# Decoder trunk: one 512-column pass of each weight tile's high part over both activation parts

## Chip, core and metric

The kernel runs on one core of a Trainium2 chip. Its engines are TensorE (PE, with weight loads shown apart as PEld), VectorE (DVE), ScalarE (ACT), GpSimd (POOL) and SyncE (SP, which only issues DMAs here). Each takes its instructions in the order in which they stand on it; semaphores tie them together. The metric is the device time of one execution in microseconds, the median of several runs.

## What is computed

Two layers of a hybrid decoder block over 256 tokens of 1024 features, float32 in and out:

```python
def reference(x, mem, positions, ...):          # x (1, 256, 1024), mem (1, 256, 1024)
    for l in range(2):
        h = rmsnorm(x, norm_mix[l])
        x = x + mixer_block(h, ...)             # below
        x = x + cross_attention(rmsnorm(x, ...), rmsnorm(mem, ...), wq, wk, wv, wo)   # 4 heads
        x = x + squared_relu_mlp(rmsnorm(x, ...), w_up, w_down)                       # 4096 hidden
    return rmsnorm(x, norm_final)

def mixer_block(h, ...):
    zin = h @ w_in                              # 6840 columns: operands of four mixers, and gates
    o_a = mla_branch(...)                       # latent attention, causal
    o_b = spatial_gating_branch(...)            # gMLP
    o_c = gla_branch(...)                       # gated linear attention
    o_d = deltanet_branch(...)                  # short convolution, triangular solve
    proj = einsum('bsnw,nwd->bsnd', branches, w_branch)
    gate = sigmoid(gates).reshape(b, s, 4, 1024)
    return sum(gate * proj, axis=2) @ w_out
```

## The kernel before

**Products.** Activations lie feature-major: 128 features on the partitions, 256 tokens along the free axis, so that a weight tile of 128 x 128 is loaded into TensorE and 256 columns of activations pass over it. Every float32 operand is split into a high part that float32r holds exactly and a low part, the rest. `mm3` (L176 to L179) makes one product of three matmuls: high weights with high activations (L177), high weights with low activations (L178), low weights with high activations (L179). The low x low product is left out.

**Weights.** `half` (L156) hands out the weight stream: 1 MB loads by SyncE into three raw buffers, each of two halves; a half is eight tiles of 128 x 128. ScalarE rounds a half to `wh` (L172), VectorE subtracts to get `wl` (L173); four buffers of each.

**Loops.** `gemm` (L181) runs over pairs of blocks of 128 output features, and in a block over the k-tiles of 128 input features (8, or 32 in the MLP's down product). A pair shares one PSUM bank of three (`pg`, tiles named g). With `lead` the first pair, with `tail` the last pair goes into banks of their own. A function `evac` takes the result away: for the gates one ScalarE tanh over 512 elements (L1043), for the MLP's up product a VectorE maximum, a ScalarE square and a split (L1164 to L1174), for products that go back into `x` a VectorE add (L335), and for keys, queries and others a ScalarE copy and a VectorE subtraction (`split_ps`). `gemm_tok` makes token-major products with 512 columns per matmul.

**Memory.** Working tiles come from a pool of 44 pieces of 2080 bytes per partition. `new` takes the piece that has been free longest (`free.pop(0)`), `rel` puts it at the end of the list. This happens in the program's order; a tile's first write then waits for the last use of what was in its piece. The gates of the first four output blocks (`gates(0)` to `gates(3)`) have tiles of their own (`gate_tile`), those of the last four take pieces.

**Order.** The program is written layer by layer: input projection, then `soft_gates`, `conv`, the rest of the projection, then two chains that take turns (DeltaNet: `dn_system`, `dn_solve`, `dn_out`; and gMLP, MLA, GLA one after the other), then eight `gates(m)`, the operands of `mem`, the keys of the cross-attention (tiles kx), eight `merge(m)`, the output product, cross-attention and MLP. A list scheduler then sets the order of instructions on each engine: whatever is ready goes first, so matmuls of the gates, which need nothing from the mixers, are placed between the steps of the mixers' chains. `urgent` and the priorities `HP` and `WP` move some instructions ahead. That order is fixed when the program is built.

Names in the chains: `head_out` (L715) norms and gates a branch's output (`sq`, `rb`, small tiles dn..), `out_branch` (L409) splits it (`brh`, `brl`, L411 and L412). In GLA, `cum` holds cumulated decays, `dd` their differences (GpSimd L788, ScalarE L789), `kt` and `qt` the scaled keys and queries of seven levels, L827 the score products, L837 to L841 the masked copies into `sc`. In DeltaNet L622 to L648 is the solve, L658 to L691 the outputs.

Of the kernel before, what the change touches and what calls it, by code (L numbers as in the profile page):

```python
# [24 lines left out]
# columns of the combined input projection  # L25
# [15 lines left out]
# pieces of on-chip memory (2080 bytes per partition each)  # L41
N_PIECE = 44
# [3 lines left out]
# constants  # L46
# [7 lines left out]
def decoder(ctx: ExitStack, tc: tile.TileContext, ws, xt_d, mem_d, pos_d, nrm_d, par_d, cst_d, msk_d, out_d):  # L54
# [26 lines left out]
    free = list(range(N_PIECE))  # L81
    owner = {}

    def new(dt=F32, shape=(P, 2, T), name="a"):
        assert free, "no piece left: " + str(sorted(n for _, _, n in owner.values()))
        i = free.pop(0)
        t = ap.tile(list(shape), dt, tag=f"pc{i}", name=nm(name))
        owner[id(t)] = (i, t, name)
# [23 lines left out]
    hh = [cp.tile([P, 2, T], F32R, name=f"hh{j}") for j in range(4)]  # L112
    hl = [cp.tile([P, 2, T], F32R, name=f"hl{j}") for j in range(4)]
# [4 lines left out]
    # first loads: x between the parts of the first weights  # L118
# [62 lines left out]
    def gemm(xh, xl, nk, npair, evac, lead=False, tail=False):  # L181
        """feature-major product, two blocks of 128 output features at a time; evac gets (blocks, psum) parts.
        lead: the first two blocks go side by side, for operands that are still being made.
        tail: the last two blocks in banks of their own, to be taken one by one."""
        for p in range(npair):
            apart = (lead and p == 0) or (tail and p == npair - 1)
            if apart:
                bk = [pg.tile([P, 2, T], F32, tag="g", name=nm("g")) for _ in range(2)]
                parts = [(slice(m, m + 1), bk[m][:, 0:1]) for m in range(2)]
                out = [bk[m][:, 0] for m in range(2)]  # L190
            else:
                ps = pg.tile([P, 2, T], F32, tag="g", name=nm("g"))
                parts = [(slice(0, 2), ps)]
# [7 lines left out]
            for m, k in order:  # L201
# [3 lines left out]
                mm3(out[m], w[m][0][:, c], w[m][1][:, c], xh(k), xl(k), k == 0, k == nk - 1)  # L205
            evac(p, parts)

    def ch(tiles):
        return lambda k: tiles[k // 2][:, k % 2, :]

    def gemm_tok(xh, xl, evac):
        """token-major product with 512 columns: out[t] = x[t]^T w"""
        ps = [pg.tile([P, 512], F32, tag="g", name=nm("g")) for _ in range(2)]
        for f in range(4):
            wh, wl = half()
            for kk in range(2):
                k = 2 * f + kk
                c = slice(512 * kk, 512 * kk + 512)
                for t in range(2):
                    s = slice(128 * t, 128 * t + 128)  # L220
                    mm3(ps[t], xh(k)[:, s], xl(k)[:, s], wh[:, c], wl[:, c], k == 0, k == 7)
# [18 lines left out]
    def rsqrt2(src, scale, eps, name):  # L240
        """the same for two columns, as two chains that take turns"""
# [15 lines left out]
    def row_of(cols, out=None, name="row"):  # L257
        """columns [128, 2] (token-major) -> [128, 256], the same row on every partition"""
# [54 lines left out]
    def gate_tile(i, dt=F32, name="gt"):  # L313
        return ap.tile([P, 2, T], dt, tag=f"gt{i}", name=nm(name))

    def operands(j, g, mix=False, parts=(slice(0, 2),)):
        if mix and parts[0].start == 0:
            if j == 0:
                Norm.h, Norm.l = [], []
            Norm.h.append(gate_tile(2 * j, F32R, "xh")), Norm.l.append(gate_tile(2 * j + 1, F32R, "xl"))  # L320
        if g is not None:
            dh, dl = (Norm.h[j], Norm.l[j]) if mix else (hh[j], hl[j])
# [3 lines left out]
    def residual(g, mix=False, row=None):  # L326
        @urgent
        def evac(p, parts):
            for c, ps in parts:
                if row is not None:  # L330
                    t = new(name="rt")
                    V.tensor_tensor(t[:, c], ps, bc2(row, c.stop - c.start), op=ALU.mult)
                    ps = t[:, c]
                    rel(t)
                V.tensor_tensor(xs[p][:, c], ps, xs[p][:, c], op=ALU.add)  # L335
                operands(p, g, mix, (c,))
            sumsq(p, xs[p], [c for c, _ in parts], g is None)
            if g is None:
                Norm.xg = [new(name="xg")] if p == 0 else Norm.xg + [new(name="xg")]
                for c, _ in parts:  # L340
# [56 lines left out]
    def layer(l):  # L397
# [5 lines left out]
        # values that pass between the parts of a layer  # L403
# [3 lines left out]
        brh, brl = [None] * 4, [None] * 4  # L407

        def out_branch(n, src):  # L409
            brh[n], brl[n] = new(F32R, name="brh"), new(F32R, name="brl")  # L410
            S.copy(brh[n], src)  # L411
            V.tensor_tensor(brl[n], src, brh[n].bitcast(F32), op=ALU.subtract)  # L412

        H, L = ch(hh), ch(hl)
# [953 lines left out]
```

## Time and profile before

| | before |
|---|---|
| median of 3 runs | 1117.18 us (1116.73 to 1117.33) |
| span of the profiled execution, its first to its last instruction | 1114.9 us |
| mean granted TensorE clock | 0.996 |
| ScalarE busy | 588.4 us |
| GpSimd busy | 185.7 us |
| DMA | 184.68 MB, mean 166 GB/s |

The profiled execution has no time of its own beside its span; the median of the runs is 2.3 us longer than that span. L12 stands for line 12 of the kernel; a line can be that of a helper, so all feature-major products have the lines 177 to 179. `x105` counts instructions. A matmul's duration overlaps that of the next one, since matmuls are pipelined; float32 matmuls outside the products appear twice in the trace for one in the program.

### The profile page before, as it was taken

What the parts mean: (1) busy time and instruction counts of PE and PEld (TensorE: products, weight loads), DVE (VectorE), ACT (ScalarE), POOL (GpSimd) and SP (SyncE); (2) the same over time, 40 slices, a digit from 0 to 9 for tenths busy, and PEclk for the clock granted to TensorE, in tenths of its full rate; (3) what the DMA queues carried; (4) which work ended last, traced back from release to release, by engine and by line L of the source; (5) the groups of instructions that cost most, each with busy time, mean ns of one, the idle gap of its engine ahead of it and who ended that gap; (6) DMA issues with size and microseconds to landing.
All of it is one profiled execution on the core that took longest, in us unless ns stands there. A gap on an engine that the chain in (4) does not pass through costs nothing.

```text
span 1114.9 us, 21506 instructions
## 1 busy us (share of the span) xinstructions
PE 1095.4 (98%) x8894; PEld 1070.2 (96%) x8894; DVE 811.1 (73%) x1415; ACT 588.4 (53%) x883; POOL 185.7 (17%) x173
## 2 busy tenths in 40 slices
PE   7999999999999999999999999999999999999996
PEld 7999999999999999999999999999999899999996
DVE  6999858868875866655689996686796777665543
ACT  6575555644654655544455646545454555554441
POOL 2233014108200200000102320410450010000010
PEclk9999999999999999999999999999999999999998
DMA  8454424454543555555545343344555344555541
GB/s 318 176 190 149 152 77 142 162 171 170 190 151 114 192 187 189 188 180 183 180 176 200 136 162 140 107 150 160 178 180 178 147 145 165 184 187 189 190 152 38
DMA packets 28035, 184.68 MB, mean 166 GB/s; under 512 B 3488, under 2 KB 3744, under 8 KB 6560
## 3 DMA queue, kind: packets, MB, share of 16 engines
q1 hardware_dynamic: 26784, 181.19, 45.6%
q10 hardware_dynamic: 1152, 2.10, 0.7%
q8 instruction: 70, 1.15, 0.4%
q14 instruction: 29, 0.24, 0.1%
HBM read 182.23 MB, written 1.05 MB: 164 GB/s over the span
## 4 chain that ended last, share of the span: by engine, by line
PE 93%; DVE 4%; ACT 1%; issue 1%; DMA 0%; POOL 0%; SPq 0%; DVEq 0%
PE g L177 27%; PE g L178 27%; PE g L179 27%; PE ps L827 1%; DVE wl L173 1%; PE ps L177 1%; PE ps L178 1%; PE ps L179 1%; PE ps L622 1%; PE ps L626 1%; DMA x<-xt 0%; ACT wh L172 0%; PE ps L933 0%; DVE hn L449 0%; PE ps L742 0%
## 5 line engine op out<-in xcount | busy, mean ns | idle before, releaser
L173 DVE TENSOR_TENSOR wl<-wr,wh 128x1024 fp32r<-128x1024 f32 (+1 forms) x338 | 414.0, 1227 | 188.5 <-ACT wh L172 184.3
L172 ACT ACTIVATE wh<-wr 128x1024 fp32r<-128x1024 f32 (+1 forms) x338 | 355.0, 1053 | 363.8 <-PE g L178 314.1
L179 PE MATMUL g<-hh,wl 128*128 128x256 f32 x1280 | 363.8, 285 | 1.4 <-DVE wl L173 1.4
L177 PE MATMUL g<-hh,wh 128*128 128x256 f32 x1280 | 363.4, 285 | 0.0
L178 PE MATMUL g<-hl,wh 128*128 128x256 f32 x1280 | 362.9, 284 | 0.0
L179 PEld LDWEIGHTS g<-hh,wl 128*128 128x128 f32 x1280 | 245.0, 192 | 2.5 <-DVE wl L173 1.8
L178 PEld LDWEIGHTS g<-hl,wh 128*128 128x128 f32 x1280 | 245.3, 192 | 0.7 <-issue 0.5
L177 PEld LDWEIGHTS g<-hh,wh 128*128 128x128 f32 x1280 | 245.0, 192 | 0.6 <-issue 0.2
L178 PE MATMUL g<-al,wh 128*128 128x256 f32 x512 | 144.1, 281 | 0.0
L177 PE MATMUL g<-ah,wh 128*128 128x256 f32 x512 | 144.0, 281 | 0.0
L179 PE MATMUL g<-ah,wl 128*128 128x256 f32 x512 | 144.0, 281 | 0.0
L179 PEld LDWEIGHTS g<-ah,wl 128*128 128x128 f32 x512 | 96.5, 188 | 0.0
L177 PEld LDWEIGHTS g<-ah,wh 128*128 128x128 f32 x512 | 96.4, 188 | 0.0
L178 PEld LDWEIGHTS g<-al,wh 128*128 128x128 f32 x512 | 96.4, 188 | 0.0
L291 POOL TENSOR_TENSOR sq<-sq,sq 128x512 f32<-128x512 f32 x16 | 23.6, 1474 | 408.6 <-ACT sq L285 408.5
L177 PE MATMUL g<-xh,wh 128*128 128x256 f32 x160 | 46.2, 293 | 6.9 <-ACT wh L172 6.9
L1059 POOL TENSOR_TENSOR gt<-gt,gt 128x512 f32<-128x512 f32 x16 | 35.7, 2228 | 99.3 <-DVE gt L1058 98.4
L178 PE MATMUL g<-xl,wh 128*128 128x256 f32 x160 | 46.2, 291 | 0.7 <-DVE xl L271 0.7
L179 PE MATMUL g<-xh,wl 128*128 128x256 f32 x160 | 46.1, 290 | 0.0
L177 PEld LDWEIGHTS g<-xh,wh 128*128 128x128 f32 x160 | 31.5, 199 | 7.0 <-ACT wh L172 6.9
L1167 DVE TENSOR_SCALAR up<-g 128x512 f32<-128x512 f32 (+1 forms) x34 | 22.5, 660 | 20.8 <-PE g L179 20.6
L177 PE MATMUL g<-brh,wh 128*128 128x256 f32 x128 | 36.3, 284 | 0.3
(467 smaller groups left out, 2100.5 us busy)
## 6 DMA issues: line engine op xcount, KB each, us to landing
wr<-ws SPq DMA_DIRECT2D x167, 1024.0 KB, 4.8
mr<-memt ACTq DMA_DIRECT2D x8, 256.0 KB, 3.2
par<-par SPq DMA_DIRECT2D x2, 778.0 KB, 7.1
x<-xt SPq DMA_DIRECT2D x4, 256.0 KB, 6.3
wr<-ws SPq DMA_DIRECT2D x2, 512.0 KB, 5.4
yt<-xg SPq DMA_DIRECT2D x4, 256.0 KB, 2.3
cst<-cst SPq DMA_DIRECT2D x1, 588.0 KB, 8.8
msk<-msk SPq DMA_DIRECT2D x1, 448.0 KB, 9.1
```

What stands on the lines that cost most here:

```text
L172: S.activation(wh[:, p], r[:, p], AF.Copy)
L173: V.tensor_tensor(wl[:, p], r[:, p], wh[:, p].bitcast(F32), op=ALU.subtract)
L177: PE.matmul(out, ah, bh, start=start, stop=False)
L178: PE.matmul(out, ah, bl, start=False, stop=False)
L179: PE.matmul(out, al, bh, start=False, stop=stop)
L291: G.tensor_tensor(acc, acc, sq, op=ALU.add)
L622: PE.matmul(xp[:, h], M[:, h], Tm[:, h], start=True, stop=True)
L626: PE.matmul(up[:, h], X[t][:, h], U[:, h], start=True, stop=True)
L827: PE.matmul(lp[:, 4 * t : 4 * t + 4], kt[i // 2][:, i % 2, 128 * t : 128 * t + 128], qt[:, :, 64 * t : 64 * t + 64], start=True, stop=True,)
L1059: G.tensor_tensor(gt[m][0], gt[m][0], gt[m][1], op=ALU.add)
L1167: V.tensor_scalar(t[:, c], ps, 0.0, None, op0=ALU.max)
```

## The change

Activations' high and low parts now lie side by side in one tile (`pair`, shape P x 2 x 2 x T: part, k, token), so that one matmul of 512 columns passes both over `wh` into the two halves of a bank; a second matmul of 256 columns passes the high part over `wl` and adds to the first half. Each block of 128 output features has a bank of its own. `add_ps` joins the two halves: a ScalarE copy of one, a VectorE add of the other. This form (`wide=True`) holds for the gates, keys, output, query, cross-attention output, up and down products; their `lead` and `tail` pairs, the input projection, the token-major products and the small products stay with `mm3`. The pool has 22 pieces of twice the size; a `pair` takes a whole one, `new` half of one, and a piece is free again only when both of its halves are. The gate tiles become four double ones, shared by the two tiles of a gate.

```diff
-N_PIECE = 44
+N_PIECE = 22
+W_HALF = 520
...
+    def pair(name):
+        p = Piece(F32R, (P, 2, 2, T), name)
...
     def new(dt=F32, shape=(P, 2, T), name="a"):
-        i = free.pop(0)
-        t = ap.tile(list(shape), dt, tag=f"pc{i}", name=nm(name))
+        p = opened.pop(dt, None)
+        o = W_HALF
+        if p is None:
+            p, o = Piece(dt, (P, 2 * W_HALF), name), 0
+            opened[dt] = p
+        p.users += 1
...
-            free.append(owner.pop(id(t))[0])
+            p = owner.pop(id(t))[0]
+            p.users -= 1
+            if p.users == 0:
+                free.append(p.i)
...
+            if wide and not apart:
+                for m in range(2):
+                    ps = pg.tile([P, 2, T], F32, tag="g", name=nm("g"))
+                    for k in range(nk):
+                        if k % 8 == 0:
+                            wh, wl = half()
+                        c = slice(128 * (k % 8), 128 * (k % 8) + 128)
+                        PE.matmul(ps, wh[:, c], x(k), start=k == 0, stop=False)
+                        PE.matmul(ps[:, 0], wl[:, c], x(k)[:, 0], start=False, stop=k == nk - 1)
+                    evac(p, [(slice(m, m + 1), ps[:, 0:1], ps[:, 1:2])])
+                continue
...
+    def add_ps(out, a, b):
+        S.copy(out, b)
+        V.tensor_tensor(out, a, out, op=ALU.add)
...
         def gates(m):
+            g2 = gate_tile(m) if m < 4 else None
             def evac(a, parts):
-                ps = parts[0][1]
-                if m < 4:
-                    t = gate_tile(2 * m + a)
-                else:
-                    t = new(name="gt")
-                S.activation(t, ps, AF.Tanh, scale=0.5)
-                gt[m][a] = t
-            gemm(H, L, 8, 2, evac)
+                (c, ps, more), = parts
+                if c.start == 0:
+                    gt[m][a] = g2[:, a] if m < 4 else new(name="gt")
+                t = gt[m][a]
+                add_ps(t[:, c], ps, more)
+                if c.stop == 2:
+                    S.activation(t, t, AF.Tanh, scale=0.5)
+            gemm(H, 8, 2, evac, wide=True)
...
         def ev_up(p, parts):
-            t = new(name="up")
-            for c, ps in parts:
-                V.tensor_scalar(t[:, c], ps, 0.0, None, op0=ALU.max)
-            S.activation(t, t, AF.Square)
-            a, b = new(F32R, name="ah"), new(F32R, name="al")
-            S.copy(a, t)
-            V.tensor_tensor(b, t, a.bitcast(F32), op=ALU.subtract)
+            for c, ps, more in parts:
...
+                if more is not None:
+                    add_ps(t[:, c], ps, more)
...
+            if parts[-1][0].stop == 2:
+                V.scalar_tensor_tensor(t, t, 0.0, t, op0=ALU.max, op1=ALU.mult)
+                ax.append(pair("ax"))
+                split_ps(ax[p][:, 0], ax[p][:, 1], t)
```

What this does to the order is shown at three places. Lines shift: L177 to L179 become L206 to L208, the wide pass is L225, the narrow one L226, `wh` and `wl` L201 and L202, the copy and the add of `add_ps` L400 and L401, L404 is the copy of a split.

First, PE in the MLP's up product of layer one, two k-tiles of a block, before (hh and hl are the two parts of the activations):

```order
L177 MATMUL g_4873<-hh_80,wh_4876 128x256
L178 MATMUL g_4873<-hl_84,wh_4876 128x256
L179 MATMUL g_4873<-hh_80,wl_4877 128x256
L177 MATMUL g_4873<-hh_80,wh_4876 128x256
L178 MATMUL g_4873<-hl_84,wh_4876 128x256
L179 MATMUL g_4873<-hh_80,wl_4877 128x256
L177 MATMUL g_4873<-hh_81,wh_4876 128x256
L178 MATMUL g_4873<-hl_85,wh_4876 128x256
```

and now (hx holds both parts):

```order
L225 MATMUL g_4213<-hx_80,wh_4216 128x512
L226 MATMUL g_4213<-hx_80,wl_4217 128x256
L225 MATMUL g_4213<-hx_80,wh_4216 128x512
L226 MATMUL g_4213<-hx_80,wl_4217 128x256
L225 MATMUL g_4213<-hx_81,wh_4216 128x512
L226 MATMUL g_4213<-hx_81,wl_4217 128x256
```

Two matmuls stand where three stood, one of them twice as wide. Over the whole program 3456 matmuls of 256 columns go and 1728 of 512 come.

Second, PE in layer one at GLA's scores (qt and kt into ps, L827; L742 belongs to `head_out`), before:

```order
L177 MATMUL g_2531<-hh_81,wh_2562 128x256
L178 MATMUL g_2531<-hl_85,wh_2562 128x256
L742 MATMUL ps_1614<-cst,rb_1612 128x128 [waits PE_49,Activation_49]
L742 MATMUL ps_1614<-cst,rb_1612 128x128 x3
L827 MATMUL ps_1629<-qt_1624,kt_1464 128x256 [waits PE_49]
L827 MATMUL ps_1629<-qt_1624,kt_1464 128x256
L827 MATMUL ps_1639<-qt_1634,kt_1465 128x256 x2
L827 MATMUL ps_1649<-qt_1644,kt_1465 128x256 [waits PE_49]
L827 MATMUL ps_1649<-qt_1644,kt_1465 128x256
L827 MATMUL ps_1659<-qt_1654,kt_1466 128x256 x2
L179 MATMUL g_2531<-hh_81,wl_2563 128x256
L177 MATMUL g_2531<-hh_82,wh_2562 128x256
```

and now (the scores are L883), up to the first gate matmul after them:

```order
L883 MATMUL ps_1594<-qt_1589,kt_1418 128x256 [waits DVE_49]
L883 MATMUL ps_1594<-qt_1589,kt_1418 128x256
L883 MATMUL ps_1604<-qt_1599,kt_1419 128x256 [waits DVE_49]
L883 MATMUL ps_1604<-qt_1599,kt_1419 128x256
L883 MATMUL ps_1614<-qt_1609,kt_1419 128x256 [waits DVE_49,PE_49]
L883 MATMUL ps_1614<-qt_1609,kt_1419 128x256
L883 MATMUL ps_1624<-qt_1619,kt_1419 128x256 [waits PE_49]
L883 MATMUL ps_1624<-qt_1619,kt_1419 128x256
L225 MATMUL g_2152<-hx_80,wh_2153 128x512 [waits DVE_49]
L226 MATMUL g_2152<-hx_80,wl_2154 128x256
```

Before, g_2531 is the fourteenth of the sixteen pairs of gate blocks (its 48 matmuls run around the scores), and there are gate matmuls between nearly all steps of the chains. Now g_2152 is the twentieth of 32 single blocks; the nineteenth, g_2127, stands before L687 (L631 before), and between the two there are 75 rows of mixer matmuls and none of a gate.

Third, ScalarE at the same place. Before, evictions of the gates (gt<-g, L1043) are spread through the chain:

```order
L172 ACTIVATE wh_2562<-wr_2532 128x1024 [waits PE_49]
L723 ACTIVATE sq_1572<-dz_740 128x512 [waits PE_49,Activation_49]
L1043 ACTIVATE gt_2407<-g_2348 128x512 [waits PE_49]
L172 ACTIVATE wh_2595<-wr_2593 128x1024 [waits DMAHW6_49,PE_49]
L172 ACTIVATE wh_2623<-wr_2593 128x1024 [waits PE_49]
L738 COPY rb_1612<-dny_1586 128x512 [waits DVE_49]
```

and now (br is the DeltaNet branch, mr the loads of `mem`; gt_2100 is the tile of gate 4, the first that comes from the pool):

```order
L779 ACTIVATE sq_1519<-og_660 128x512 [waits PE_49,Activation_49]
L794 COPY rb_1558<-dny_1533 128x512 [waits DVE_49]
L404 CAST br_1566<-sq_1519 128x512 [waits DVE_49]
L1136 DMA mr_2473<-memt 128x512 [waits DVE_49]
L1136 DMA mr_2481<-memt 128x512
L400 COPY gt_2100<-g_2077 128x256 [waits PE_49]
L400 COPY gt_2100<-g_2103 128x256
L400 COPY gt_2100<-g_2127 128x256
```

The three banks filled before the stretch are copied out behind the DeltaNet branch and two loads, in a row; the piece of gt_2100 last held `qt` tiles of GLA. In layer two the same rows stand in the same order.

More of the change, by code (lines that the diff above doesn't have):

```diff
@@ L111, in decoder @@
     xs = [cp.tile([P, 2, T], F32, name=f"x{j}") for j in range(4)]
-    hh = [cp.tile([P, 2, T], F32R, name=f"hh{j}") for j in range(4)]
-    hl = [cp.tile([P, 2, T], F32R, name=f"hl{j}") for j in range(4)]
+    hx = [cp.tile([P, 2, 2, T], F32R, name=f"hx{j}") for j in range(4)]
     cs = cp.tile([P, T], F32, name="cs")
@@ L405, in layer @@
             pass
-        brh, brl = [None] * 4, [None] * 4
+        br = [None] * 4
         def out_branch(n, src):
[L410 to L414, printed above, removed]
+            br[n] = pair("br")
+            split_ps(br[n][:, 0], br[n][:, 1], src)
+        H = ch(hx)
         zc = []
@@ L433, in ev_dn @@
                 z = R.gkv = new(name="gkv")
-            for c, ps in parts:
+            for c, ps, _ in parts:
                 if p == 0:
@@ L872, in mla @@
             V.tensor_scalar(rsq, rm[:, 0:2], 96.0**-0.5, None, op0=ALU.mult)
[L873 removed]
+            cqx = pair("cqx")
+            cqh, cql = cqx[:, 0], cqx[:, 1]
             split_scaled(cq, col(PC_NQ, 2), cqh, cql)
@@ L1078, in layer @@
                 sumsq(j, mr)
-            a, b = new(F32R, name="mh"), new(F32R, name="ml")
-            split_scaled(mr, gain(4 * l + 2)[:, 2 * j : 2 * j + 2], a, b)
-            mh.append(a), ml.append(b)
+            mx.append(pair("mx"))
+            split_scaled(mr, gain(4 * l + 2)[:, 2 * j : 2 * j + 2], mx[j][:, 0], mx[j][:, 1])
             rel(mr)
@@ L1085, in layer, with ev_split @@
             row_of(rsm, out=rowm)
[L1087 removed]
+        def ev_split(xs_, name):
             def evac(p, parts):
[L1089 to L1096 removed]
+                for c, ps, more in parts:
+                    if c.start == 0:
+                        xs_.append(pair(name))
+                    if more is not None:
+                        if c.start == 0:
+                            R.sum = new(name="sum")
+                        add_ps(R.sum[:, c], ps, more)
+                        if c.stop == 2:
+                            split_ps(xs_[-1][:, 0], xs_[-1][:, 1], R.sum)
+                            rel(R.sum)
+                    else:
+                        split_ps(xs_[-1][:, 0, c], xs_[-1][:, 1, c], ps)
+            return evac
+        kx = []
+        gemm(ch(mx), 8, 4, ev_split(kx, "kx"), wide=True)
         for m in range(8):
             merge(m)
[L1100 to L1103 removed]
+        rel(br)
+        gemm(ch(mg), 8, 4, residual(gain(4 * l + 1)), lead=True, tail=True, wide=True)
+        rel(mg)
         rs = stat("rsx")
         V.tensor_scalar(rs, rs, 1.0 / 16, None, op0=ALU.mult)
[L1108 to L1110 removed]
+        qx = []
+        gemm(H, 8, 4, ev_split(qx, "qx"), lead=True, wide=True)
         px = [[None] * 2 for _ in range(2)]
@@ L1161, in layer @@
         rrow = row_of(rs, name="rrow")
-        ah, al = [], []
+        ax = []
         def ev_up(p, parts):
-            t = new(name="up")
-            for c, ps in parts:
-                V.tensor_scalar(t[:, c], ps, 0.0, None, op0=ALU.max)
-            S.activation(t, t, AF.Square)
-            a, b = new(F32R, name="ah"), new(F32R, name="al")
-            S.copy(a, t)
-            V.tensor_tensor(b, t, a.bitcast(F32), op=ALU.subtract)
-            ah.append(a), al.append(b)
-            rel(t)
-        gemm(H, L, 8, 16, ev_up, lead=True)
-        gemm(ch(ah), ch(al), 32, 4, residual(gain(4 * l + 4), True, rrow) if l + 1 < NL else residual(None, False, rrow), tail=True)
-        rel(ah, al)
+            for c, ps, more in parts:
+                if c.start == 0:
+                    R.up = new(name="up")
+                t = R.up
+                if more is not None:
+                    add_ps(t[:, c], ps, more)
+                else:
+                    S.copy(t[:, c], ps)
+            if parts[-1][0].stop == 2:
+                V.scalar_tensor_tensor(t, t, 0.0, t, op0=ALU.max, op1=ALU.mult)
+                ax.append(pair("ax"))
+                split_ps(ax[p][:, 0], ax[p][:, 1], t)
+                rel(t)
+        gemm(H, 8, 16, ev_up, lead=True, wide=True)
+        last = residual(gain(4 * l + 4), True, rrow) if l + 1 < NL else residual(None, False, rrow)
+        gemm(ch(ax), 32, 4, last, tail=True, wide=True)
+        rel(ax)
     for j in range(4):
```

121 lines of the change are left out of this document (66 added, 55 removed).

## The prediction

> **What bounds the kernel now.** First the page: the span, the busy shares, the chain that ended last.
>
> ```profile
> span 1114.9 us, 21506 instructions
> PE 1095.4 (98%) x8894; PEld 1070.2 (96%) x8894; DVE 811.1 (73%) x1415; ACT 588.4 (53%) x883; POOL 185.7 (17%) x173
> ...
> PE 93%; DVE 4%; ACT 1%; issue 1%; DMA 0%; POOL 0%; SPq 0%; DVEq 0%
> ```
>
> TensorE is busy 1095.4 of 1114.9 us and holds 93% of the chain. A busy PE can hide waits, so second the view of waits, for PE alone (waiter, releaser, us in total, times, longest):
>
> ```profile
> PE g L177 <- ACT wh L172: 6.9, 1, 6.9
> PE ps L1194 <- DVE rsfiny L253: 2.1, 1, 2.1
> ```
>
> These, its longest, are the first weights and the final norm. Between them PE waits for almost nothing: the kernel is a stream of matmuls, and the latency chains of the mixers run beside gate products that keep PE fed. So two things can move the time: what a matmul costs, and whether PE always has one to issue. Third, PE's timeline gives the cost by columns: the first and last of 41 starts in a row with 256 columns, then of 23 with 512 (the token-major products).
>
> ```profile
> 600.00 0.28 PE L177 MATMUL g<-hh,wh 128*128 128x256 f32 x1
> ...
> 604.80 0.28 PE L178 MATMUL g<-hl,wh 128*128 128x256 f32 x1
> ```
>
> ```profile
> 325.21 0.40 PE L178 MATMUL g<-wl,mh 128*128 128x512 f32 x1
> ...
> 330.33 0.39 PE L179 MATMUL g<-wh,ml 128*128 128x512 f32 x1
> ```
>
> A duration overlaps the next instruction's; the step between starts is the price: 4.80/40 = 0.120 us for 256 columns, 5.12/22 = 0.2327 us for 512.
>
> **Term 1: the wide passes.** Between the two programs 3456 matmuls of 256 columns go and 1728 of 512 come; the `wl` pass stays. By the rows a k-step goes from 3 x 0.120 = 0.360 us to 0.2327 + 0.120 = 0.353. That saves 0.0073 us per wide pass, 1728 x 0.0073 = **12.6 us** in all. No row shows wide and narrow passes in turn. If a wide pass costs as much as two narrow ones the gain is 0; if the narrow pass that follows hides the 0.0073 that doesn't grow with columns a second time, it is 25 us. I take 12.6: its rows are the same instruction in this kernel.
>
> One rule speaks of just this price. The Trainium skill, "TensorE: Matmul & The Clock Gate", section "Back-to-back issue gap", gives a sustained 131 ns per matmul of 512 columns; by it the term would be an estimated 1728 x (240 - 131) ns = 188 us. The row here has 232.7 ns, and the measurement decides.
>
> **Term 2: evictions.** Each wide block (180 of them: per layer 84 of eight k-steps and 6 of thirty-two) now needs a ScalarE copy of one half and a VectorE add of the other before its bank is free.
>
> ```profile
> 390.59 0.37 ACT L264 COPY rrow<-ps 128x256 f32<-128x256 f32 x1 [0.22 <-PE ps L261]
> ```
>
> ```profile
> L173 DVE TENSOR_TENSOR wl<-wr,wh 128x1024 fp32r<-128x1024 f32 (+1 forms) x338 | 414.0, 1227 | 188.5 <-ACT wh L172 184.3
> L172 ACT ACTIVATE wh<-wr 128x1024 fp32r<-128x1024 f32 (+1 forms) x338 | 355.0, 1053 | 363.8 <-PE g L178 314.1
> ```
>
> ```profile
> L335 DVE TENSOR_TENSOR x<-g,x 128x256 f32<-128x256 f32 x16 | 6.5, 416 | 8.5 <-PE g L179 8.5
> ```
>
> ```profile
> 200.34 0.69 DVE L745 TENSOR_TENSOR sq<-ps,sq 128x512 f32<-128x512 f32 x1
> ```
>
> A block of eight steps takes PE 8 x 0.353 = 2.82 us; with three banks a bank must be back two blocks, 5.6 us, later. At worst the copy stands behind one `wh` (1.05) and takes 0.37, and the add behind a `wl` and two 512-element operations (1.23 + 0.69 + 0.69) and takes 0.42: 4.5 us. It fits. In the MLP's up product VectorE does 2 x 1.23 + 2 x 0.42 + 2 x 0.69 = 4.7 us per pair of blocks in 5.6. So PE's next two blocks hide it, price 0; without that cover a block would cost copy and add in series, 0.8 us, 180 x 0.8 = 144 us, and a part of that is a rival below.
>
> **Term 3: the filler goes.** This lies in the order, not in the arithmetic. The gate products fill PE while the mixers' chains run. Gates 0 to 3 have tiles of their own; gates 4 to 7 take pieces, handed out first-freed first. With 22 double pieces in place of 44, the piece of gate 4 is one that held a late `qt` tile of GLA. So in the order of the change the last gate block is g_2127; then come all mixer steps from L687 (L631 before) to the last score product L883 (L827), and no gate matmul between. The copies that free the banks stand on ScalarE behind the DeltaNet branch (L404) and two loads of `mem` that wait for VectorE. Layer two has the same order. In the kernel before, the same stretch is 148.9 to 207.9 us: in the view by stretches all engines (after the length: PE, PE's weight loads, DVE, ACT, POOL busy, clock, DMA), from its start and from `cum` on, then VectorE's `wl` line alone from there, then the view of the tile g for one of its three lines.
>
> ```profile
> 148.90:207.90 59.00, 59.00 (x499) 56.44 (x499) 43.39 (x103) 30.41 (x50) 16.29 (x16) 1.00 0.36 123
> 163.20:207.90 44.70, 44.70 (x357) 43.02 (x357) 39.57 (x99) 23.06 (x35) 16.29 (x16) 1.00 0.41 138
> ```
>
> ```profile
> 163.20:207.90 44.70, 12.67 (x10) 1.00 0.41 138
> ```
>
> ```profile
> L177 PE MATMUL g<-hh,wh x105: 274/283/466, 150.7 to 207.6; 128*128 128x256 f32 x105
> ```
>
> 315 gate matmuls (105 for each of three lines) at 0.120 are 37.8 us of the 59.0; the mixers' own matmuls are the other 21.2. In the change the 37.8 us are done elsewhere, where PE was full already, and here PE idles for the stretch's new length less 21.2. It gets shorter, since nothing queues behind filler. Upper bound: at the old 59.0, PE idles 37.8. Lower bound: `cum`, at 163.2 before, cannot come sooner than that less the filler ahead of it (57 matmuls, 6.8 us), 7.5 us into the stretch, and VectorE then has 39.57 - 12.67 = 26.9 us besides `wl`: 34.4, so 13.2 idle. Between them I walk the chain with the durations of before:
>
> ```profile
> 150.40 1.56 ACT L949 COPY pt<-ps 128x512 f32<-128x512 f32 x3
> ...
> 196.16 0.62 ACT L738 COPY rb<-dny 128x512 f32<-128x512 f32 x1
> ```
>
> ```profile
> 164.20 5.57 POOL L788 TENSOR_SCALAR dd<-dd 128x512 f32<-128x512 f32 x3 [18.93 <-DVE dd L787]
> ...
> 179.10 0.73 POOL L683 TENSOR_TENSOR qe<-qe,cv 128x256 f32<-128x256 f32 x1 [1.42 <-ACT qe L682]
> 182.68 2.09 POOL L807 TENSOR_TENSOR sc<-cst,dg 128x512 f32<-128x512 f32 x2 [2.85 <-DVE dg L803]
> ```
>
> ```profile
> 188.41 0.17 DVE L731 TENSOR_TENSOR dnm<-ps,r8y 128x8 f32<-128x8 f32 x1 [1.19 <-PE ps L722]
> ...
> 195.96 0.17 DVE L735 SCALAR_TENSOR_TENSOR dny<-dny,r8y 128x8 f32<-128x8 f32 x1
> ...
> 203.67 2.77 DVE L841 COPY_PREDICATED sc<-msk,ps 128x256 f32<-128x256 int32 x8
> ```
>
> ```profile
> L822 DVE TENSOR_TENSOR qt<-dd,qbd x28: 274/280/1126, 168.3 to 185.0; 128x128 f32<-128x128 f32 x28
> ```
>
> ```profile
> 199.41 0.89 PE ps L742 x8
> ```
>
> Leg one, to GpSimd's first `dd`: 164.2 - 148.9 = 15.3 us before, 8.5 without the filler; I take 10.5, since three `pt` copies (1.56) and a `wh` (1.05) stand in ScalarE's queue ahead of the solve's copies. Leg two, GpSimd to the end of `qe`: 179.83 - 164.20 = 15.6 before; GpSimd's 16.29 less the two `sc` after it (2.09) is 14.2. Leg three, from there to the add that frees a bank: 26.6 before, to the end of the masked copies at 206.44. Now: output matmuls and column sums (each about as long as L742's 0.89), copy (a third of the 1.56), square (as L738, 0.62), together 2.9; the norm's small steps 195.96 + 0.17 - 188.41 = 7.7 less two `wl` of 1.23, 5.3; row copy (L738) 0.62, transposes 0.89, product (L745) 0.69, 2.2; the branch's subtraction (another 0.69), eight `qt` multiplies (8 x 0.28), eight masked copies (2.77) and the add (0.42), 6.2; some twenty hops between engines, 1.2; 17.8 in all. The sum is 42.5 us, so PE idles 42.5 - 21.2 = 21.3, rounded up to **22 us per layer**, for the walk leaves out small steps.
>
> TensorE also comes back slow from such holes:
>
> ```profile
> 13.22 0.41 PE L178 MATMUL g<-xl,wh 128*128 128x256 f32 x1
> 13.43 0.41 PE L179 MATMUL g<-xh,wl 128*128 128x256 f32 x1
> ```
>
> ```profile
> 1103.00:1108.00 5.00, 1.48 (x10) 1.19 (x10) 3.45 (x20) 0.51 (x1) 0.00 (x0) 0.80 0.00 0
> 1108.00:1115.00 7.00, 0.92 (x4) 0.62 (x3) 2.48 (x4) 0.00 (x0) 0.00 (x0) 0.50 0.40 150
> ```
>
> At the program's start matmuls still step at 0.21 us so late as this, some 5 us after the first; at its end, once PE has little to do, the granted clock falls to 0.50. Nothing lost is one bound; 5 us at half rate, 2.5 us, the other; I take **2 us per layer**, near the second, since the hole is longer than the 5 us at the end. The sum: -12.6 + 2 x (22 + 2) = +35.4. The profiled execution is known by its span, 1114.9, which becomes 1150.3; the runs' median lies 2.3 us above that span, unchanged, so 1117.2 + 35.4 = **1152.6 us**.
>
> **The rivals.**
> (a) *Faster: a wide pass costs clearly less than its row*, all 1728 of them. To pay for 48 us of holes it must save 27.8 ns, so it decides from 0.212 us down; at 0.200 the time is 1117.2 - 69 + 48 = 1096. Against it: 23 starts at 0.2327 on average. By the Trainium skill's rule named under term 1 the same sum gives 1117.2 - 188 + 48 = 977; the row bears it out so little that it shares this rival's chance.
> (b) *The hole keeps the old length*: queues, not filler, made the stretch 59 us. Idle 37.8 and 2.5 per layer: 1117.2 - 12.6 + 80.6 = 1185. For it: the engines work in order and the chain has many hops. Against: 12.67 us of `wl` leave VectorE's queue.
> (c) *Evictions stall PE everywhere*: 0.2 us on each of 180 blocks is 36 us, 1189 in all. Against it 4.5 of 5.6 us; for it the mixers' part, where VectorE is fullest.
> (d) *The hole is as short as VectorE's bound*: 1117.2 - 12.6 + 2 x 13.2 = 1131; with 25 us from term 1, 1119.
>
> **How the numbers follow.** A hole of 17 to 33 us idle has 0.64, (d) 0.11, (b) 0.12, (c) 0.08, (a) 0.04, and 0.01 that the parts cancel. The range takes in (b), (d) and most of the price of a wide pass; it leaves out (a), most of (c) and the last ends: 1122 to 1188. Faster by over 0.2% (about what a measurement of this kernel can tell from no change) 0.04, within 0.01, slower 0.95.
>
> **What would show it.** Right: in each layer one hole some 43 us long, from about 155 us into the span and again in layer two, where PE's busy share falls to about half and ends in a wait on VectorE's add (L401); elsewhere PE full, a wide and a narrow pass 0.353 us together. Wrong: waits on L401 spread over all wide blocks (c); wide starts under 0.212 apart (a); a full PE through the stretch, which would say that the order does not bind.

## The result, and the profile after

The changed kernel takes **1150.84 us** (median of four runs, 1150.48 to 1152.78) where the kernel before, timed beside it, takes 1116.95. The ratio is 1.0306, with a 95% interval from 1.0294 to 1.0319: slower by 3.1%, against 1152.6 us predicted. The profiled execution took 1150.48 us, its span 1148.6.

From the page after: the span, the busy shares, the 40 slices of PE and of its granted clock, and the engines' shares of the chain.

```profile
span 1148.6 us, 18394 instructions
PE 1102.2 (96%) x7166; PEld 993.3 (86%) x7166; DVE 863.5 (75%) x1613; ACT 613.7 (53%) x1019; POOL 184.1 (16%) x173
PE   7999987999999999999999999789999999999996
PEclk9999995999999999999999999779999999999998
...
PE 87%; DVE 9%; ACT 2%; issue 1%; DMA 0%; SPq 0%; DVEq 0%; ACTq 0%
```

PE is busy 6.8 us longer than before, with fewer matmuls and 512 columns in many of them. A busy PE is not a full PE, and the slices say where: two places, one per layer, where PE thins out and its clock falls. By stretches of time (columns as in the prediction), the two places (first and last row), and two undisturbed stretches between them:

```profile
160.20:202.30 42.10, 30.07 (x184) 24.95 (x184) 26.00 (x86) 12.02 (x27) 15.30 (x20) 0.68 0.07 25
202.30:260.00 57.70, 57.70 (x352) 50.62 (x353) 41.61 (x84) 37.52 (x64) 5.83 (x5) 1.00 0.50 171
420.00:560.00 140.00, 140.00 (x814) 122.76 (x813) 97.33 (x125) 70.98 (x102) 3.65 (x3) 1.00 0.54 188
722.60:764.70 42.10, 30.02 (x184) 25.25 (x184) 25.89 (x85) 11.78 (x27) 15.28 (x20) 0.68 0.09 32
```

Each hole lasts 42.1 us, and in it PE runs the 184 matmuls of the mixers and no gate product. In the third row (the MLP) PE never stops, though each wide block there has a copy and an add at its end. The waits of PE agree: none is on the add, L401, not even at a hole's end, where the last score product still counts as busy when the gate matmul is about to start. The longest four:

```profile
PE ps L798 <- ACT rb L794: 8.4, 2, 4.2
PE g L206 <- ACT wh L201: 7.7, 1, 7.7
PE ps L730 <- DVE r L726: 5.4, 2, 2.7
PE ps L723 <- DVE uu L720: 4.1, 2, 2.1
```

But for the second, the first weights at the program's start, these waits are the mixers' own latency, bare now. PE's timeline has a hole's beginning, its middle and its end, and ScalarE's and VectorE's timelines what ends it:

```profile
160.12 0.65 PE L687 MATMUL ps<-X,U 64*64 64x32 f32 x8
...
177.13 1.94 PE L730 MATMUL ps<-r,U 128*128 128x64 f32 x8 [2.68 <-DVE r L726]
...
195.61 6.61 PE L883 MATMUL ps<-qt,kt 128*128 128x256 f32 x24
202.27 0.50 PE L225 MATMUL g<-hx,wh 128*128 128x512 f32 x1
```

```profile
199.93 0.87 ACTq L1136 DMA_DIRECT2D mr<-memt  x2
200.84 0.92 ACT L400 COPY gt<-g 128x256 f32<-128x256 f32 x3 [3.63 <-DVE sc L897]
```

```profile
201.80 0.75 DVE L401 TENSOR_TENSOR gt<-g,gt 128x256 f32<-128x256 f32 x2
```

Three finished gate blocks have stood in their banks. Their copies run from 200.84 on, directly behind the two loads of `mem` (L1136), whose issuing takes ScalarE until 200.80 and which in the chain that ended last follow a masked copy. The first of two adds ends at about 202.2, and the next gate matmul starts at 202.27. PE's last score product starts at 201.84, and these products step by 0.22 us, so PE waits for the add for only some 0.2 us. In layer two it doesn't wait at all: there the add ends at 764.53, the last two score products start at 764.39, and the gate matmul follows on them at 764.64. So a hole ends when two chains are through, the copies with their add and the score products that stand ahead of the gate block on PE, and they end almost together. Last, the pace in the MLP, from PE's timeline:

```profile
429.71 0.40 PE L225 MATMUL g<-hx,wh 128*128 128x512 f32 x1
...
433.95 0.40 PE L225 MATMUL g<-hx,wh 128*128 128x512 f32 x1
```

Between them lie twelve k-steps of a wide and a narrow pass: 4.24 / 12 = 0.353 us each.

### The profile page after: what moved, and what is told of

Its sections match the earlier page's. It is cut to its first block, busy times and chain, and to the rows that moved or that the text cites. A ratio compares the mean times of both kernels' runs of the same rounds, so it can differ in the third digit from the quotient of the medians.

```text
span 1148.6 us, 18394 instructions
## 1 busy us (share of the span) xinstructions
PE 1102.2 (96%) x7166; PEld 993.3 (86%) x7166; DVE 863.5 (75%) x1613; ACT 613.7 (53%) x1019; POOL 184.1 (16%) x173
## 3 DMA queue, kind: packets, MB, share of 16 engines
HBM read 182.23 MB, written 1.05 MB: 160 GB/s over the span
## 4 chain that ended last, share of the span: by engine, by line
PE 87%; DVE 9%; ACT 2%; issue 1%; DMA 0%; SPq 0%; DVEq 0%; ACTq 0%
PE g L225 34%; PE g L226 18%; PE g L206 8%; PE g L207 8%; PE g L208 8%; DVE wl L202 2%; PE ps L207 1%; PE ps L208 1%; PE ps L206 1%; ACT wh L201 1%; DVE cv L556 1%; PE ps L678 1%; PE ps L682 1%; PE ps L883 1%; PE ps L798 1%
## 5 line engine op out<-in xcount | busy, mean ns | idle before, releaser
L202 DVE TENSOR_TENSOR wl<-wr,wh 128x1024 fp32r<-128x1024 f32 (+1 forms) x338 | 416.3, 1233 | 175.9 <-ACT wh L201 173.2
L201 ACT ACTIVATE wh<-wr 128x1024 fp32r<-128x1024 f32 (+1 forms) x338 | 355.4, 1054 | 356.7 <-PE g L225 164.3
L225 PE MATMUL g<-hx,wh 128*128 128x512 f32 x1088 | 384.8, 397 | 0.0
L226 PE MATMUL g<-hx,wl 128*128 128x256 f32 x1088 | 306.8, 282 | 1.6 <-DVE wl L202 1.6
L225 PEld LDWEIGHTS g<-hx,wh 128*128 128x128 f32 x1088 | 204.2, 188 | 47.1 <-DVE gt L401 0.4
L226 PEld LDWEIGHTS g<-hx,wl 128*128 128x128 f32 x1088 | 205.5, 189 | 3.1 <-DVE wl L202 2.8
L225 PE MATMUL g<-ax,wh 128*128 128x512 f32 x384 | 134.8, 394 | 0.0
L226 PE MATMUL g<-ax,wl 128*128 128x256 f32 x384 | 108.0, 281 | 0.0
L225 PEld LDWEIGHTS g<-ax,wh 128*128 128x128 f32 x384 | 72.1, 188 | 16.8
L226 PEld LDWEIGHTS g<-ax,wl 128*128 128x128 f32 x384 | 72.3, 188 | 0.0
L208 PE MATMUL g<-hx,wl 128*128 128x256 f32 x192 | 53.7, 284 | 0.8 <-DVE wl L202 0.8
L207 PE MATMUL g<-hx,wh 128*128 128x256 f32 x192 | 54.3, 285 | 0.0
L206 PE MATMUL g<-hx,wh 128*128 128x256 f32 x192 | 53.8, 284 | 0.0
L206 PE MATMUL g<-xm,wh 128*128 128x256 f32 x160 | 46.0, 292 | 7.7 <-ACT wh L201 7.7
L207 PE MATMUL g<-xm,wh 128*128 128x256 f32 x160 | 46.2, 291 | 0.6 <-DVE xm L313 0.6
L208 PE MATMUL g<-xm,wl 128*128 128x256 f32 x160 | 46.0, 290 | 0.0
L225 PE MATMUL g<-mx,wh 128*128 128x512 f32 x128 | 45.0, 394 | 0.0
L206 PEld LDWEIGHTS g<-xm,wh 128*128 128x128 f32 x160 | 31.4, 199 | 7.7 <-ACT wh L201 7.7
L206 PE MATMUL g<-br,wh 128*128 128x256 f32 x128 | 37.3, 291 | 0.6 <-DVE gt L1118 0.6
L208 PEld LDWEIGHTS g<-hx,wl 128*128 128x128 f32 x192 | 36.5, 192 | 1.2 <-DVE wl L202 1.2
```

The lines of the kernel that those rows point to most:

```text
L201: S.activation(wh[:, p], r[:, p], AF.Copy)
L202: V.tensor_tensor(wl[:, p], r[:, p], wh[:, p].bitcast(F32), op=ALU.subtract)
L206: PE.matmul(out, ah, bh, start=start, stop=False)
L207: PE.matmul(out, ah, bl, start=False, stop=False)
L208: PE.matmul(out, al, bh, start=False, stop=stop)
L225: PE.matmul(ps, wh[:, c], x(k), start=k == 0, stop=False)
```

## The experiments

Four theories stand behind the expectations. **P**: the loss is the tile of gate 4, which waits for a piece that GLA still holds. **B**: a wide gate block fills a bank with 128 features where a narrow pair fills it with 256, so three banks hold less work. **S**, formed after the second set of runs: the order is planned as if a 512-column matmul took no longer than a 256-column one. **W**: wide passes and their evictions cost time wherever they stand. A question by itself is what the low clock in the hole costs. Times are medians; before is 1116.6 to 1117.3 in all sets.

### The pool without the wide passes

```diff
-            if wide and not apart:
+            if False and wide and not apart:
...
-                add_ps(t[:, c], ps, more)
-                if c.stop == 2:
-                    S.activation(t, t, AF.Tanh, scale=0.5)
+                S.activation(t, ps, AF.Tanh, scale=0.5)
```

> The change without its wide passes: 22 double pieces, pairs and gate tiles as in the change, three 256-column matmuls per k-step and the old evictions everywhere. If the starved tile of gate 4 is the whole loss (theory P, the prediction's), only the gain of the passes goes: 1150.8 + 12.6 = 1163 us, with the hole in its place. If part of the hole comes from the banks (theory B: a wide block fills a bank with 128 features, a narrow one with 256, so three banks take 8.6 us of matmuls more before PE stalls), the hole is shorter by that in each layer: 1163 - 17 = 1146 us. If wide passes and their evictions cost the time (theory W), 1117 us.

Measured: 1136.94 us, ratio 1.0176 [1.0162, 1.0190]. None of the three numbers, and nearest to B. The pool alone costs 20 us, not 46. By stretches, the places where this kernel has no gate matmul:

```profile
177.40:203.90 26.50, 19.67 (x88) 16.15 (x87) 19.61 (x58) 5.67 (x10) 6.73 (x7) 0.61 0.20 68
736.00:757.80 21.80, 15.06 (x90) 12.49 (x88) 17.49 (x56) 5.72 (x11) 3.68 (x4) 0.84 0.19 66
```

The hole ends like the one of the change, with gate 4's first eviction, but begins 17 us later. So a second thing, in the gate blocks themselves, brings PE to gate 4 sooner.

### Four pieces kept for gates 4 to 7

```diff
-            self.i = free.pop(0)
+            self.i = (kept if kept and name == "gt" else free).pop(0)
...
+        kept.extend(free.pop(0) for _ in range(4))
```

Here and in the next two a freed half of a piece is also handed out again at once, so that 18 pieces do for the rest.

> The change with a pool that keeps four pieces for gates 4 to 7 through the mixers (a freed half of a piece is handed out again, so 18 pieces do for the rest); wide passes and evictions as in the change. P: no hole, 1117.0 - 12.6 = 1104 us. B: the order still has one run of some 22 mixer steps without a gate matmul (from L735, L730 in the change, to the fourth score product; 20 us in the trace of the change), up to 12 us idle per layer: 1105 to 1128 us. W: as the change, 1150 us.

> The same pool with the narrow passes and old evictions of the kernel before: P and B 1117 us (within 2), since PE has gate matmuls through the whole stretch; W also 1117. Above 1119 the handing out of halves costs something itself. Its distance to the run with the kept pieces and wide passes is the price of the wide passes with the same pool.

> The same pool, the 32 gate blocks of each layer narrow (256 features in a bank, evicted by the tanh alone), all other wide passes kept: 1728 - 512 = 1216 wide passes. P and B: no hole, 1117.0 - 1216 x 0.0073 = 1108 us. W: 116 of 180 wide blocks still pay, 1117 + 34 x 116/180 = 1139 us.

Measured: 1155.25 us (ratio 1.0346 [1.0332, 1.0360]), 1148.64 us (1.0285 [1.0271, 1.0299]) and 1148.33 us (1.0280 [1.0266, 1.0294]). All three missed, and even the one without a wide pass is 32 us slow. One row of PE's timeline of that one, and for the kernel before the view of the solve's first product (its first and last start in the run):

```profile
148.94 1.05 PE L683 MATMUL ps<-U,M 128*128 128x128 f32 x8
```

```profile
L622 PE MATMUL ps<-T,M x64: 270/275/275, 125.5 to 690.3; 128*128 128x128 f32 x64
```

The triangular solve starts 23 us late, with gate matmuls on PE up to it. The likely reason is that the mixers' own tiles wait for one another in the 18 recycled pieces; no run shows that by itself. The gates had their tiles and were used up early: in the first run of the three PE has no gate matmul left from 209.0 us on, and runs dry first on the mixers' own chain, then on the memory operands of the cross-attention (waits of PE):

```profile
PE ps L803 <- ACT sq L799: 13.3, 2, 6.7
...
PE g L229 <- DVE mx L317: 6.9, 5, 2.3
PE g L229 <- DVE sum L405: 5.4, 3, 2.7
```

So the scarce thing is room for work ahead, and keeping it for one user takes it from another. On wide passes they say one thing: the 1216 outside the gates save 0.3 us in this pool (1148.64 to 1148.33), where 8.9 were worked out.

### Narrow gates in the change's pool; wide gates in the old pool

```diff
-            gemm(H, 8, 2, evac, wide=True)
+            gemm(H, 8, 2, evac)
```

> The change with its own pool, but the gate blocks narrow (256 features in a bank, the tanh alone evicts); 1216 wide passes stay. B (a wide gate block fills a bank with half the features, so PE stalls sooner once gate 4 waits for its tile): the hole is that of the run with narrow passes everywhere, 1136.9 - 1216 x 0.0073 = 1128 us. P (only the tile counts): the change less the gain of 512 passes, 1150.8 + 3.7 = 1154.5 us. W (wide passes and evictions cost wherever they stand): 1137 + 14 x 116/180 = 1146 us.

Measured: 1133.76 us, ratio 1.0150 [1.0136, 1.0164]: 17 us less than the change by the gates' form alone. P by itself is out; B's 1128 is missed by 6.

In the other, the kernel before with `hh` and `hl` side by side, and only the gates wide:

```diff
+                        PE.matmul(ps, wh[:, c], x, start=k == 0, stop=False)
+                        PE.matmul(ps[:, 0], wl[:, c], x[:, 0], start=False, stop=k == nk - 1)
...
+            gemm(H, L, 8, 2, evac, wide=wide)
```

> The kernel before with its 44 single pieces; only the 64 gate blocks are wide (512 passes), with copy and add at eviction. P: the tiles are free as before, so only the gain, 1117.0 - 3.7 = 1113 us. B: the order has a run of mixer steps without a gate matmul (from L659 to L683, L643 to L667 in the kernel before), since three banks hold 8.5 us of gate matmuls: 5 to 10 us per layer, 1123 to 1133 us. W: 1117 + 14 x 64/180 = 1122 us, without such a hole.

Measured: 1138.68 us, ratio 1.0203 [1.0185, 1.0221], slower than any theory said. With single pieces as before, 64 wide gate blocks cost 21.6 us, and 25.3 if the 3.7 that their passes should gain are added. PE's timeline of the kernel before, with a product of the solve and the one that follows it; then of this one, with the solve's first product ahead of the same two:

```profile
131.60 1.06 PE L622 MATMUL ps<-T,M 128*128 128x128 f32 x8
135.61 1.05 PE L626 MATMUL ps<-U,X 128*128 128x128 f32 x8
```

```profile
134.02 1.05 PE L638 MATMUL ps<-T,M 128*128 128x128 f32 x8
...
141.33 1.06 PE L638 MATMUL ps<-T,M 128*128 128x128 f32 x8
146.27 1.05 PE L642 MATMUL ps<-U,X 128*128 128x128 f32 x8
```

The step took 4.01 us and takes 4.94: the order puts 26 narrow gate matmuls between the two there, 23 wide and narrow ones in turn here, near the same number, but 4.1 us of work for 3.1. The solve starts 8.5 us later (134.02 for 125.5), each step is slower, and the gates that have tiles are used up before the mixers free more: when the solve starts, thirteen blocks of gates have been evicted, in the kernel before ten. This fits S. The change itself has the same: 24 matmuls of the wide form between two solve steps (L678 at 140.87, L682 at 145.94, so 5.07 us). From 158.4 to 174.0 us there is then no gate matmul; the end of that gap on VectorE and ScalarE:

```profile
171.77 0.62 DVE L797 TENSOR_SCALAR dd<-cum 128x128 f32<-128x128 f32 x1
171.96 0.42 DVE L680 TENSOR_TENSOR s<-ps,cst 128x256 f32<-128x256 f32 x1
```

```profile
172.47 0.65 ACT L358 COPY gt<-g 128x256 f32<-128x256 f32 x2 [1.19 <-DVE s L680]
```

By the order in which pieces are handed out, gate 4's first tile takes over the piece of `cum`; L797 is its last reader, done at 172.39, and the copy starts at 172.47. (The view names L680, which ends at 172.38.)

### Wide passes away from the mixers

The same pool, with only the MLP's up product and the query product wide:

```diff
+        gemm(H, L, 8, 4, ev_split(qh, ql, "qx"), lead=True, wide=wide_q)
...
+        gemm(H, L, 8, 16, ev_up, lead=True, wide=wide_up)
```

> The kernel before with its 44 single pieces; only the MLP's up product and the cross-attention's query product are wide (576 passes, 72 blocks), none beside the mixers. P and B: 1117.0 - 576 x 0.0073 = 1112.8 us, faster than both kernels. W: 1117 + 14 x 72/180 = 1122.6 us. This tells the price of a wide pass and its eviction apart from everything else.

Measured: **1111.56 us, ratio 0.9950 [0.9937, 0.9962]**, faster than both kernels. W is out. The gain of 5.5 us (by the interval 4.2 to 7.0) for 576 passes fits the 4.2 worked out at its lower end.

### More pieces

```diff
-N_PIECE = 22
+N_PIECE = 24
...
-        wh = wp.tile([P, 1024], F32R, tag="wh", name=nm("wh"), bufs=4)
-        wl = wp.tile([P, 1024], F32R, tag="wl", name=nm("wl"), bufs=4)
+        wh = wp.tile([P, 1024], F32R, tag="wh", name=nm("wh"), bufs=3)
+        wl = wp.tile([P, 1024], F32R, tag="wl", name=nm("wl"), bufs=3)
```

> The change with 24 double pieces for 22 (the room comes from the split weights: three buffers each for four). P and B: gate blocks run some 10 us further into the stretch of the hole (the order has them up to L718), so the hole loses up to 8 us per layer: 1150.8 - 16 = 1135 us, down to 1150 if three weight buffers cost as much. W: 1150.8 us.

Measured: 1169.17 us, ratio 1.0475 [1.0461, 1.0489]. The room was taken from the wrong place; PE now waits for split weights (waits of PE; the first was 1.6 us in the change, the second not there):

```profile
PE g L226 <- DVE wl L202: 8.1, 6, 2.0
...
PE g L225 <- ACT wh L201: 5.5, 10, 1.0
```

Beyond that, the run tells nothing on P.

### One block a bank, narrow; tiles for gates 4 and 5

The kernel before, its gate blocks with a bank each for 128 features:

```diff
+                    ps = pg.tile([P, 2, T], F32, tag="g", name=nm("g"))
...
+                        mm3(ps[:, 0], wh[:, c], wl[:, c], xh(k), xl(k), k == 0, k == nk - 1)
+                    single(p, m, ps)
...
+                S.activation(gt[m][a][:, c], ps[:, 0], AF.Tanh, scale=0.5)
```

> The kernel before with its 44 single pieces and narrow passes; only the gate blocks take a bank each for 128 features, as the wide ones do, evicted by one tanh. B (half the features in a bank is what makes PE stall): as the wide gates without the gain, 1138.7 + 3.7 = 1142 us, with the gap of some 15 us from the mixers' triangular solve on. S (the order plans a 512-column matmul like a 256-column one, so wide gate blocks stand in front of the mixers' steps for 4.2 us at a time in place of 3.1, and use up the gates that have tiles before the mixers free more): narrow blocks keep the old pace, 1117 to 1122 us, no such gap.

Measured: 1127.95 us, ratio 1.0099 [1.0082, 1.0115]. Between the two: half-filled banks, with two evictions for one, cost some 11 us of the 25; the six runs lie between 1124.5 and 1131.2, so this is good to some 3 us. The pace of the order is the old one:

```profile
132.00 1.06 PE L632 MATMUL ps<-T,M 128*128 128x128 f32 x8
136.01 1.05 PE L636 MATMUL ps<-U,X 128*128 128x128 f32 x8
```

Again 26 narrow gate matmuls lie between the two, the step takes 4.01 us, the solve starts at 125.9 us, and ten blocks of gates have been evicted by then. So the faster use of the gates belongs to the wide form, as S has it, and not to the banks. The other 14 us come with the wide passes: the order's pace and the add at eviction, which no run parts.

Then the kernel with wide gates (1138.7 us), two more gates with tiles of their own, and four pieces fewer:

```diff
-N_PIECE = 44
+N_PIECE = 40
...
-                    gt[m][a] = gate_tile(2 * m + a) if m < 4 else new(name="gt")
+                    gt[m][a] = gate_tile(2 * m + a) if m < 6 else new(name="gt")
```

> The kernel with wide gates and single pieces (1138.7 us), where gates 4 and 5 now have tiles of their own and the pool 40 pieces for 44. P (what ends the gap from 158.4 to 174.0 us is the tile of gate 4, whose piece still holds cum): this gap goes; the order then runs out of gates with tiles later, at L683, so a part of the loss comes back there: 1117 to 1135 us. B: the gap stays where it is, 1138 us.

Measured: 1135.29 us, ratio 1.0163 [1.0150, 1.0176]. The old place of the gap, and the new one, by stretches:

```profile
158.40:174.00 15.60, 15.60 (x128) 13.52 (x128) 5.37 (x7) 9.42 (x20) 2.05 (x4) 1.00 0.35 133
189.70:211.60 21.90, 13.51 (x84) 11.27 (x83) 18.01 (x55) 7.54 (x15) 4.44 (x4) 0.77 0.20 69
```

With a tile for gate 4 PE is full there: the tile was what PE waited for, not the bank. The gap comes back 30 us later, when gates 4 and 5 are used up. Just as in the four-pieces runs, a loss cured in one place appears in the next.

### Matmuls that nobody reads, in the hole

```diff
-    pp = ctx.enter_context(tc.tile_pool(name="pp", bufs=5, space=bass.MemoryType.PSUM))
+    pp = ctx.enter_context(tc.tile_pool(name="pp", bufs=4, space=bass.MemoryType.PSUM))
...
+                for i in range(300):
+                    PE.matmul(fl[:, 0, 0:128], hx[i % 4][:, 0, 0, 0:128], hx[i % 4][:, 0, 1, 0:128], start=True, stop=True)
```

> The change with 300 matmuls of 128 columns per layer that nobody reads, put ahead of gate 4, in a PSUM bank of their own (four banks for the mixers in place of five); by the order some 260 of them stand in the hole. If the low clock in the hole comes from PE's idleness and stretches it, the granted clock there rises from 0.68 to 0.9 or more, the mixers' matmuls take their old durations (L883's about 0.9 us for eight... half of now) and the stretch from L687 to the last score product shrinks from 42.1 us by up to 6: 1138 to 1151 us. If the clock is only a symptom, the stretch stays at 42 us or grows by what the added matmuls delay: 1151 to 1165 us.

Measured: 1175.71 us, ratio 1.0526 [1.0511, 1.0541]: above both. The stretch of the hole, and from PE's timeline 24 of the added matmuls and the mixers' product that was L730 in the change:

```profile
157.50:205.00 47.50, 47.50 (x416) 44.71 (x416) 21.36 (x68) 12.92 (x25) 15.64 (x20) 1.00 0.07 24
```

```profile
161.80 2.89 PE L1135 MATMUL fl<-hx 128*128 128x128 f32 x24
164.62 0.68 PE L704 MATMUL ps<-vt,T 64*64 64x64 f32 x8
...
183.23 1.05 PE L731 MATMUL ps<-r,U 128*128 128x64 f32 x8
```

The clock stays at 1.00, and eight matmuls that took 1.94 us in the change take 1.05. So PE's idleness is what lowers the clock. What that costs can't be read from the total: the added matmuls have 128 columns, but step at 2.82 / 24 = 0.118 us, like those of 256, so 300 of them are 35 us a layer, more than the hole could take; and the mixers have one bank less.

### The change's pool with halves handed out again

```diff
-        p = opened.pop(dt, None)
...
+        if (not slots or clock[0] - slots[0][2] < 6) and free:
+            p = Piece(dt, (P, 2 * W_HALF), name)
+            slots[:0] = [(p, 0, -999), (p, W_HALF, -999)]
+        p, o, _ = slots.pop(0)
...
-            gemm(H, 8, 2, evac, wide=True)
+            gemm(H, 8, 2, evac)
```

> The change with its 22 double pieces and narrow gate blocks (1133.8 us so far), but a freed half of a piece is handed out again once six other tiles have been handed out; 1216 wide passes stay. P (what costs is that gate 4 gets a piece that GLA still holds): the order's first layer now has gate blocks through the whole stretch as in the kernel before, so 1117.0 - 8.9 = 1108 us, below both kernels, and up to 1112 for the second layer, whose order has fewer blocks there. If double pieces or the other wide products cost the 16.8 us themselves, 1134 us.

Measured: 1117.89 us, ratio 1.0009 [1.0000, 1.0018]. Against the same kernel without the handing out (1133.76) that is 15.9 us less. So the pool's part comes from how its pieces are handed out, as P says, though this edit eases every tile of the pool and not that of gate 4 alone. By stretches, where the hole of layer one stood, and that of layer two:

```profile
148.80:213.30 64.50, 63.95 (x542) 61.17 (x541) 45.29 (x104) 34.03 (x55) 18.63 (x18) 1.00 0.35 118
705.00:757.00 52.00, 48.79 (x406) 45.82 (x407) 39.04 (x103) 23.71 (x37) 17.25 (x16) 1.00 0.36 125
```

PE is full but for 0.6 and 3.2 us. The 1108 us are missed by 10; where those lie beyond the 3.2 of layer two, no run settled.

## Why the prediction came out right

**What bounds the kernel** held: whether PE always has a matmul decided it. The two holes cost 41.8 us (twice 42.1 less the mixers' 21.2), more than the whole loss of 33.9; the rest of the kernel gained 7.9.

**Term 1, the wide passes (-12.6 us): the price right, the sum not seen whole.** A k-step takes 0.353 us in the trace, as the sum had it, and 576 passes of the up and query products alone make the kernel faster by 0.50%. The 1216 passes outside the gates gain less than their 8.9 us wherever they were set against narrow ones: 3.2 us in the change's pool (1136.94 to 1133.76), 0.3 with kept pieces, and with halves handed out again the kernel is no faster than before. Which products lose it, no run settled. The rule of the Trainium skill ("TensorE: Matmul & The Clock Gate", section "Back-to-back issue gap") that would have given an estimated 188 us isn't borne out by these operands: 0.353 less a narrow pass's 0.120 leaves 0.233 us, not 0.131.

**Term 2, evictions at nothing: right in the MLP, too narrow beside the mixers.** The cover of two blocks was worked out from queues that run. Beside the mixers the copies and adds wait for a piece, the cover is what three banks hold, and a bank with half the features holds half: one block a bank costs 11 us without a copy or an add. This cost was booked nowhere under term 2; it is part of the hole.

**Term 3, the hole: its length right, with luck; its cause half right.** The walk gave 42.5 us from L687 to the add; the trace has 42.1, with no gate matmul between. It ends as named, behind the two loads and the add, but the score products on PE end with them and the wait itself is 0.2 us in layer one and none in layer two. The legs of the walk can be read from GpSimd's timeline (L844 is the first `dd`, L739 the multiply that gives `qe`):

```profile
169.72 4.96 POOL L844 TENSOR_SCALAR dd<-dd 128x512 f32<-128x512 f32 x3 [0.38 <-DVE dd L843]
...
180.53 0.72 POOL L739 TENSOR_TENSOR r<-r,cv 128x256 f32<-128x256 f32 x1 [0.86 <-ACT r L738]
```

The legs take 9.6, 11.5 and 21.0 us, where the walk had 10.5, 14.2 and 17.8. The first two were too long by 3.6 together and the third too short by 3.2; it left out the score products on PE, whose last 24 take 6.61 us. The totals cancel in the same way: the holes cost 41.8 us where the sum had 48, and the rest of the kernel gained 7.9 where it had 12.6.

The prediction laid the hole to the 22 double pieces alone. The pool alone costs 20.0 us, the wide gate blocks alone 21.6 (25.3 with the gain that their passes should bring: 11 for the banks, 14 for the passes). Put into the change's pool, the wide form of the gates adds 17.1 us to 1133.76. So about half of the 33.9 us is the gates' form, and the exact split depends on which comes first. The step that failed is the sentence that put it all on the 22 pieces in place of 44: the order was read for where the gate blocks end, and not for how fast they are used up ahead of that. It shows in the order: 26 narrow matmuls between two solve steps, and 24 of the wide form in the change, which take a third longer.

**The clock, 2 us per layer after the hole: the wrong place.** PE's clock in finer stretches of layer one's hole:

```profile
160.20:170.00 9.80, 7.58 (x88) 6.65 (x88) 3.35 (x10) 5.04 (x13) 2.26 (x5) 1.00 0.18 76
170.00:174.00 4.00, 1.62 (x7) 1.32 (x8) 4.00 (x16) 1.26 (x2) 4.00 (x3) 0.61 0.00 0
...
193.70:197.00 3.30, 3.26 (x12) 2.99 (x13) 1.14 (x4) 0.42 (x1) 0.00 (x0) 0.50 0.00 0
197.00:199.50 2.50, 2.50 (x11) 2.08 (x10) 2.50 (x8) 0.20 (x1) 0.00 (x0) 0.77 0.00 0
199.50:202.20 2.70, 2.70 (x13) 2.06 (x11) 2.70 (x10) 0.92 (x3) 0.00 (x0) 1.00 0.35 107
```

The last score products already keep PE busy from 193.7 on and pay the slow start, so the gate matmuls resume at full pace. PE is busy 30.07 us in the hole for work that was 21.2 in the prediction. Idle time and longer busy time, 12.0 and 8.9, make the 20.9 us that the walk had as idle alone. The longer busy time is the low clock and, since durations overlap on a full PE, also the ends of matmuls that stand alone; the trace doesn't part the two. That they together met the number is luck in part.

**The rivals.** (a) is out by the pace, (b) by 42.1 us for 59, (d) by the same for 34.4. (c) as it was put, a stall on every block, is out by the MLP's row; a piece of its mechanism, evictions that stand where VectorE is fullest, may be in the 14 us of the gates' wide passes, which are not parted from the order's pace.

## What to carry to other kernels

Filler work is worth what it covers: ask of a change not only what it saves per instruction, but how fast it uses up the work that runs beside a latency chain, and what that work needs to start (a tile, a bank). An order planned by other prices than the chip's spends filler early; compare time between two steps of the chain, not the number of instructions. Where a part of a change is cheap and lies away from the chain, as the wide passes of the MLP do, take that part alone.

## What the runs showed of the hardware

A matmul of these operands costs about the same with 128 columns as with 256 (0.118 and 0.120 us) and 0.233 with 512, at a granted clock of 1.00.

The granted clock fell without a long pause of PE. In stretches finer than the rows above it is 1.00 until 170.8 us and 0.50 from 170.9 on. The longest pause of PE in the hole up to there is the 1.29 us before L718, and in the 3.4 us before the fall PE shows 2.11 us busy (1.59 in layer two, before the fall at 734.0). The Trainium skill ("TensorE: Matmul & The Clock Gate", section "What's actually happening") gives an idle window of about 3.4 us for it; the trace has the fall without a whole window of silence, at a busy share of 62% (47% in layer two). The clock came back 4.4 us after PE had become busy without pauses (193.7 to 198.1), and 5.3 us after it in layer two (756.1 to 761.4).
